# Softmax sums by way of memory, and value matmuls that wait for the last transposed tile

## The chip, the cores and the metric

The kernel runs on one core of one Trainium2 chip. A core has a matmul engine (TensorE, PE in the profile; PEld is its weight load, which runs beside the matmuls), a vector engine (VectorE, DVE), an activation engine (ScalarE, ACT), GpSimd (POOL) and SyncE (SP), which here issues every transfer. The metric is the device time of one launch in microseconds (us). Three runs of the kernel before gave 2056.36, 2057.92 and 2061.26 us; the median is 2057.92.

## The reference, cut to what matters

The program is one step of a two-layer network on 256 context tokens and 1024 latent tokens. Layer A is an attention (8 heads) beside a convolution, layer C a scan over chunks. The change touches the attention's core alone:

```python
s = (einsum('bqhd,bkhd->bhqk', qn, k_nope) + einsum('bqhr,bkr->bhqk', qr, k_rope)) * ATTN_SCALE
p = softmax(s, axis=-1)
o = einsum('bhqk,bkhd->bqhd', p, v)
```

Context tokens attend to the 256 context keys only; latent tokens attend to 512 cached keys and 1024 latent keys. The result of each head is multiplied by a gate before the output projection.

## The kernel before, in words

The program is written as a flow of tile operations. A planner then orders them for each engine: where several are ready at a simulated moment, the one that comes first in the program's text goes first. The engines run their queues strictly in the planned order.

The attention is cut into 80 units: 4 pairs of heads (p), 5 blocks of 256 queries (b; block 0 is the context), 2 heads (j) of the pair, 2 halves (qi) of 128 queries. Four units with the same p and b form a group, whose outputs are stored together; 4 groups are of the context (256 keys, one segment), 16 are full (1536 keys, three segments of 512).

`u_scores` (L599) makes one unit's scores: three matmuls per segment through `mm3` (L118), a maximum on DVE (L617), the exponential on ACT, which also sums (L626), and the sum's reciprocal `ri` on DVE (L630, L631), one value per query, queries on partitions. `u_trans` (L636) transposes the probabilities in packs of four 128x128 blocks (L646) and copies each pack out of PSUM into a `ptile`, on DVE the middle pack (L650), on ACT the others (L652). `u_values` (L655) multiplies the transposed probabilities with the values. The two heads stand in the two column halves of the array and of the PSUM tile `po`: these matmuls use 128 rows by 64 columns (128*64 in the profile), where all others around them use 128*128. A matmul of 32-bit floats shows as two instructions, so a full group has 24 key tiles by heads, 48 value instructions, and a context group 8.

The result lies with queries along the free axis, so the reciprocals must be turned and repeated over the head's 64 rows. Before, TensorE does that, too, in the second half of `po` (L659 to L662), by matmuls of a broadcast `ri` with the identity: 4 matmuls, 8 instructions a group. DVE then multiplies gate and reciprocals (L671), and the values by that (L672); the product goes to memory (L673). Buffers that bind: 5 PSUM banks for scores, 2 for transposes, 1 for `po`; 2 buffers of `prob`; 7 of `ptile`, of which a full group holds 6.

The main loop (L700 to L720) issues the scores of unit i, then the transposes of unit i-1, then, where i mod 4 is 1, the values of the group that ended two units earlier. So in the text the values of a group stand behind the scores of the second unit, and the transposes of the first unit, of the next group. `prep_pair` makes keys and queries of the next pair, with transfers from memory; `conv_norm` finishes the convolution in pieces between the units, mostly on POOL.

Of the kernel before, what the change touches and what calls it, by code (L numbers as in the profile page):

```python
# [10 lines left out]
F32 = mybir.dt.float32  # L11
# [39 lines left out]
def body(nc, tc, d, dbg=None, stop=None):  # L51
    es = ExitStack()
    with es:
        _body(nc, tc, d, es, dbg or {}, stop)


def _body(nc, tc, d, es, dbg, stop):
    V, S, G, PE = nc.vector, nc.scalar, nc.gpsimd, nc.tensor
    dma = nc.sync.dma_start

    def pool(name, bufs=1, space=None, side=None, stack=es):
        kw = {}
        if space is not None:
            kw["space"] = space
        if side is not None:
            kw["side"] = side
        if space is None:
            kw["reuse_waits"] = "tile"
        return stack.enter_context(tc.tile_pool(name=name, bufs=bufs, **kw))
# [5 lines left out]
    sm = pool("sm", bufs=3, side="left")  # L75
# [9 lines left out]
    dp = pool("dp", space=DRAM)  # L85

    def psum(tag="x"):
        tag = tag if tag in ptags else "sd"
        p, n = ptags[tag]
        return p.tile([128, 512], F32, name="ps" + tag, tag=tag, bufs=n)  # L90
# [5 lines left out]
    ident = cp.tile([128, 128], F32, name="ident")  # L96
# [21 lines left out]
    def mm3(ps, lh, ll, rh, rl, start, stop_):  # L118
        PE.matmul(ps, lh, rh, start=start, stop=False)  # L119
        PE.matmul(ps, lh, rl, start=False, stop=False)  # L120
        PE.matmul(ps, ll, rh, start=False, stop=stop_)  # L121

    def after(ins, other):
        tc.add_manual_dep(ins.ins, other.ins.name,
                          mybir.DependencyInfo(mybir.DependencyClass.Sync, mybir.DependencyReason.DATA), reason="group")
# [374 lines left out]
    ap_ = pool("attn", bufs=2, side="right", stack=esB)  # L500
# [9 lines left out]
    vt = ap_.tile([128, 14, 512], F32, name="vt", bufs=1)  # L510
# [82 lines left out]
    for p in range(4):  # L593
        for b in range(5):
            for j in range(2):
                for qi in range(2):
                    units.append((p, b, j, qi))

    def u_scores(u, kq):  # L599
        p, b, j, qi = u  # L600
        ks, qs = kq
        tok = (0 if b == 0 else 256 + 256 * (b - 1)) + 128 * qi
        ci = 0 if tok < 256 else (1 if tok < 768 else 2)
        o = tok - CHUNKS[ci][0]
        segs = [0] if b == 0 else [1, 2, 3]
        qh, ql = qs[(j, ci)]
        mx = sm.tile([128, 4], F32, name="mx", tag="mx", bufs=6)
        sums = sm.tile([128, 4], F32, name="sums", tag="sums", bufs=6)
        nk = sum(KSEG[si][1] for si in segs)
        prob = ap_.tile([128, 1536], F32, name="prob", tag="prob")  # L610
        pss = []
        for x, si in enumerate(segs):
            n = KSEG[si][1]
            kh, kl = ks[(j, si)]
            ps = psum("s")
            mm3(ps[:, :n], qh[:, o:o + 128], ql[:, o:o + 128], kh[:, :n], kl[:, :n], True, True)
            V.tensor_reduce(mx[:, x:x + 1], ps[:, :n], axis=AX.X, op=ALU.max, negate=len(segs) == 1)  # L617
            pss.append((ps, n))
        if len(segs) > 1:
            nm = sm.tile([128, 1], F32, name="nm", tag="nm", bufs=6)  # L620
            V.tensor_reduce(nm, mx[:, :len(segs)], axis=AX.X, op=ALU.max, negate=True)  # L621
        else:
            nm = mx[:, 0:1]
        c = 0
        for x, (ps, n) in enumerate(pss):
            S.activation(prob[:, c:c + n], ps[:, :n], AF.Exp, bias=nm, accum_out=sums[:, x:x + 1])  # L626
            c += n
        ri = sm.tile([128, 1], F32, name="ri", tag="ri", bufs=8)
        if len(segs) > 1:
            V.tensor_reduce(ri, sums[:, :len(segs)], axis=AX.X, op=ALU.add)  # L630
            V.reciprocal(ri, ri)  # L631
        else:
            V.reciprocal(ri, sums[:, 0:1])
        return prob, ri, nk

    def u_trans(u, st, pts):  # L636
        p, b, j, qi = u
        prob, ri, nk = st
        for g in range(0, nk // 128, 4):
            n4 = min(4, nk // 128 - g)  # L640
            if qi == 0:
                pts[(j, g)] = ap_.tile([128, 4, 256], F32, name="ptile", tag="pt", bufs=7)
            dst = pts[(j, g)]
            ps = psum("pt")
            for x in range(n4):
                PE.transpose(ps[:, x * 128:(x + 1) * 128], prob[:, (g + x) * 128:(g + x + 1) * 128], ident)  # L646
            o = dst[:, :n4, qi * 128:qi * 128 + 128]
            p3 = ps[:, :n4 * 128].rearrange("p (k q) -> p k q", q=128)
            if g == 4:
                V.tensor_copy(o, p3)  # L650
            else:
                S.copy(o, p3)  # L652
        pts[("r", j, qi)] = ri

    def u_values(p, b, pts):  # L655
        q0 = 0 if b == 0 else 256 + 256 * (b - 1)
        kts = list(range(2)) if b == 0 else list(range(2, 14))
        po = psum("po")
        for qi in range(2):  # L659
            for j in range(2):  # L660
                PE.matmul(po[64 * j:64 * j + 64, 256 + 128 * qi:384 + 128 * qi],
                          pts[("r", j, qi)].to_broadcast([128, 64]), ident, start=True, stop=True)  # L662
        for x, kt in enumerate(kts):
            for j in range(2):
                h = 2 * p + j
                PE.matmul(po[64 * j:64 * j + 64, 0:256], vt[:, kt, 64 * h:64 * h + 64],  # L666
                          pts[(j, 4 * (x // 4))][:, x % 4, :], start=x == 0, stop=x == len(kts) - 1)
        t2 = ap_.tile([128, 256], F32, name="t2", tag="t2")
        sg = sgs.pop((p, b))
        om = ap_.tile([128, 256], F32, name="om", tag="om")  # L670
        V.tensor_mul(t2, sg, po[:, 256:512])  # L671
        V.tensor_mul(om, po[:, 0:256], t2)  # L672
        dma(mixd[p, :, q0:q0 + 256], om)  # L673

# [25 lines left out]
    for i in range(len(units) + 2):  # L700
        if i < len(units):
            u = units[i]
            if i % 4 == 0:
                sgs[u[:2]] = ap_.tile([128, 256], F32, name="sg", tag="sg")
                dma(sgs[u[:2]], sgd[u[0], :, 256 * u[1]:256 * u[1] + 256])
            state[u] = u_scores(u, kqs[u[0]])
            if i % 20 == 19 and u[0] < 3:
                kqs[u[0] + 1] = prep_pair(u[0] + 1)
        if 0 < i <= len(units):
            v = units[i - 1]  # L710
            pts = done.setdefault((v[0], v[1]), {})
            u_trans(v, state.pop(v), pts)
            if v[2] == 1 and v[3] == 1:
                late_v.append(v)
        if i % 4 == 1 and late_v:
            v = late_v.pop(0)
            u_values(v[0], v[1], done.pop((v[0], v[1])))
        if ci < len(cn) and i % 20 in (1, 3, 5, 7, 9, 11, 13):
            next(cn[ci])
            ci += 1  # L720
        if i == 68:
            esE.close()
            esA.close()
            wps[0] = pool("wpB", bufs=2, side="left")
            hls.append(pool("hlB0", bufs=16, side="left", stack=esH))
            load_mix(0, KORD[:4])
            wao.extend(split_w(d["wao"][m], 8, 128) for m in range(2))
# [161 lines left out]
    def dtile(name, dt=F32, tag=None):  # L889
        return dq.tile([128, HT], dt, name=name, tag=tag or name)  # L890
# [40 lines left out]
    p = dtile("p")  # L931
# [43 lines left out]
    for half in range(2):  # L975
        hs = slice(half * 64, half * 64 + 64)
        for c0 in range(0, 5):
            c = half * 5 + c0
# [561 lines left out]
```

## Time and profile before

| | us |
|---|---|
| median of three runs | 2057.92 |
| the profiled execution, its own time | 2060.95 |
| its span (first to last instruction) | 2059.1 |
| PE busy, of the span | 1993.4 (97%) |
| DVE busy | 1415.9 (69%) |
| ACT busy | 882.3 (43%) |
| POOL busy | 578.7 (28%) |

The mean granted TensorE clock is 0.988 of full speed. PE's busy time counts a matmul from its start to a modelled end, and neighbours overlap; time that PE loses between two instructions can so be hidden in it. The start times in the timeline show it: the distance from one start to the next, less what the instructions need when they follow each other densely.

### The profile page before, as it was taken

The numbers are of one execution on the slowest core, as the hardware profiler recorded it, in microseconds if no ns is written. First come the engines' busy times: TensorE is split into PE (matmuls) and PEld (weight loads), VectorE is DVE, ScalarE is ACT, GpSimd is POOL, SyncE is SP. The second block draws the span as 40 slices with busy tenths as digits, with TensorE's granted clock in tenths as the row PEclk, the third lists the DMA queues.
The fourth block names the chain that finished last, engine by engine and source line by source line (L and its number), as shares of the span: only waits on it lengthen the run. The fifth ranks groups of instructions, "written<-read, shape, count | busy, mean of one in ns | idle before, by whom it ended". The sixth has DMA issues, their size and how long they took to land.

```text
span 2059.1 us, 32474 instructions
## 1 busy us (share of the span) xinstructions
PE 1993.4 (97%) x11830; PEld 1626.0 (79%) x11830; DVE 1415.9 (69%) x2257; ACT 882.3 (43%) x1683; POOL 578.7 (28%) x487
## 2 busy tenths in 40 slices
PE   6999999999999999989999999999999999799997
PEld 3787888777777777868888888888888888589997
DVE  5798798556666673275757876876778587784744
ACT  5411321666566673244544343443334244333531
POOL 1211122212222311563123333333433243342001
PEclk8999999999999999999999999999999999999998
DMA  8434213311122224331566768765866678755442
GB/s 315 181 118 150 54 70 108 115 57 42 57 60 60 77 82 164 140 114 52 142 217 205 229 203 237 208 191 173 244 204 194 179 235 252 220 182 185 145 157 72
DMA packets 273341, 313.57 MB, mean 152 GB/s; under 512 B 21184, under 2 KB 221920, under 8 KB 273184
## 3 DMA queue, kind: packets, MB, share of 16 engines
q1 hardware_dynamic: 273184, 311.51, 48.0%
q8 instruction: 94, 1.54, 0.3%
q14 instruction: 63, 0.52, 0.1%
HBM read 223.38 MB, written 88.05 MB: 151 GB/s over the span
## 4 chain that ended last, share of the span: by engine, by line
PE 90%; DVE 3%; DMA 2%; ACT 1%; issue 1%; SPq 1%; POOL 0%; DVEq 0%; ACTq 0%; POOLq 0%
PE psmm L119 18%; PE psmm L120 18%; PE psmm L121 18%; PE pspo L666 5%; PE pspt L646 4%; PE pssd L1078 3%; PE pss L119 3%; PE pssd L1159 3%; PE pss L121 3%; PE pss L120 3%; PE pssd L1164 2%; PE pssd L1136 2%; PE pssd L1139 2%; PE psx L229 1%; PE pstm L1036 1%
## 5 line engine op out<-in xcount | busy, mean ns | idle before, releaser
L119 PE MATMUL psmm<-hl,wh 128*128 128x512 f32 (+1 forms) x1152 | 428.1, 372 | 4.7 <-ACT wh L114 3.5
L121 PE MATMUL psmm<-hl,wl 128*128 128x512 f32 (+1 forms) x1152 | 423.5, 368 | 4.3 <-POOL wl L115 4.3
L120 PE MATMUL psmm<-hl,wh 128*128 128x512 f32 (+1 forms) x1152 | 423.3, 367 | 0.0
L115 POOL TENSOR_TENSOR wl<-ws,wh 128x1024 fp32r<-128x1024 f32 x89 | 223.6, 2514 | 516.7 <-ACT wh L114 424.5
L119 PEld LDWEIGHTS psmm<-hl,wh 128*128 128x128 f32 x1152 | 219.1, 190 | 37.6 <-ACT wh L114 4.5
L121 PEld LDWEIGHTS psmm<-hl,wl 128*128 128x128 f32 x1152 | 218.8, 190 | 36.9 <-POOL wl L115 6.2
L120 PEld LDWEIGHTS psmm<-hl,wh 128*128 128x128 f32 x1152 | 218.8, 190 | 29.6 <-issue 0.7
L383 DVE SCALAR_TENSOR_TENSOR cacc<-cvin,acw,cacc 128x1295 f32<-128x1295 f32 x120 | 206.9, 1740 | 4.6 <-ACT cacc L378 3.1
L114 ACT CAST wh<-ws 128x1024 fp32r<-128x1024 f32 x109 | 113.6, 1043 | 199.6 <-PE psmm L120 140.3
L848 DVE SCALAR_TENSOR_TENSOR cy<-raw,prm,cy 128x1282 f32<-128x1282 f32 x96 | 157.2, 1637 | 24.6 <-ACT cy L845 17.0
L120 PE MATMUL psmm<-hlo,wh 128*128 128x512 f32 (+3 forms) x480 | 172.1, 359 | 0.0
L119 PE MATMUL psmm<-hh,wh 128*128 128x512 f32 (+3 forms) x480 | 167.8, 360 | 2.5 <-ACT hh L259 2.0
L121 PE MATMUL psmm<-hh,wl 128*128 128x512 f32 (+3 forms) x480 | 170.1, 357 | 0.0
L617 DVE TENSOR_REDUCE mx<-pss 128x1 f32<-128x512 f32 (+1 forms) x208 | 137.3, 668 | 35.2 <-PE pss L121 34.2
L1083 POOL TENSOR_TENSOR st<-st,dec_bc 128x256 f32<-128x256 f32 x104 | 84.3, 815 | 245.2 <-DVE st L1085 165.9
L119 PE MATMUL psmm<-yh,wh 128*128 128x256 f32 (+1 forms) x476 | 147.8, 314 | 5.2 <-ACT yh L1203 3.1
L120 PE MATMUL psmm<-yl,wh 128*128 128x256 f32 (+1 forms) x476 | 148.0, 312 | 0.4 <-DVE yl L1204 0.4
L121 PE MATMUL psmm<-yh,wl 128*128 128x256 f32 (+1 forms) x476 | 147.1, 313 | 0.0
L626 ACT ACTIVATE prob<-pss,nm 128x512 f32<-128x512 f32 x192 | 130.3, 693 | 16.1 <-DVE nm L621 14.2
L646 PE MATMUL pspt<-ident,prob 128*128 128x128 f32 x800 | 121.7, 278 | 4.9 <-ACT prob L626 3.9
L652 ACT COPY ptile<-pspt 128x512 f32<-128x512 f32 (+1 forms) x144 | 81.2, 569 | 104.8 <-PE pspt L646 104.0
L646 PEld LDWEIGHTS pspt<-ident,prob 128*128 128x128 f32 x800 | 92.1, 141 | 40.4 <-ACT prob L626 10.2
(337 smaller groups left out, 4084.5 us busy)
## 6 DMA issues: line engine op xcount, KB each, us to landing
xa<-cmb SPq DMA_DIRECT2D x80, 384.0 KB
wm<-in_wmod_dram SPq DMA_DIRECT2D x48, 512.0 KB
ws<-in_wc_dram SPq DMA_DIRECT2D x40, 512.0 KB
eb<-eyd SPq DMA_DIRECT2D x160, 128.0 KB
ws<-in_wco_dram SPq DMA_DIRECT2D x32, 512.0 KB
cmb<-xt SPq DMA_DIRECT2D x24, 640.0 KB
bx<-cmb SPq DMA_DIRECT2D x72, 192.0 KB
eb<-cmb SPq DMA_DIRECT2D x80, 128.0 KB
```

Source lines behind the costliest of these rows:

```text
L114: S.copy(wh, ws)
L115: (eng or G).tensor_sub(wl, ws, f32(wh))
L119: PE.matmul(ps, lh, rh, start=start, stop=False)
L120: PE.matmul(ps, lh, rl, start=False, stop=False)
L121: PE.matmul(ps, ll, rh, start=False, stop=stop_)
L383: V.scalar_tensor_tensor(cacc[i], cv[:, k:k + CO], acw[:, 31 * i + k:31 * i + k + 1], cacc[i], ALU.mult, ALU.add)
L617: V.tensor_reduce(mx[:, x:x + 1], ps[:, :n], axis=AX.X, op=ALU.max, negate=len(segs) == 1)
L626: S.activation(prob[:, c:c + n], ps[:, :n], AF.Exp, bias=nm, accum_out=sums[:, x:x + 1])
L646: PE.transpose(ps[:, x * 128:(x + 1) * 128], prob[:, (g + x) * 128:(g + x + 1) * 128], ident)
L666: PE.matmul(po[64 * j:64 * j + 64, 0:256], vt[:, kt, 64 * h:64 * h + 64], pts[(j, 4 * (x // 4))][:, x % 4, :], start=x == 0, stop=x == len ...
L848: V.scalar_tensor_tensor(y, raw[:, k:k + RO], ccw[:, 5 * blk + k:5 * blk + k + 1], y, ALU.mult, ALU.add)
L1083: G.tensor_mul(n.rearrange("p (h e) -> p h e", e=64), s.rearrange("p (h e) -> p h e", e=64), dec_ap(u, dr, c))
```

## The change

The matmuls that turn the reciprocals are gone. The four reciprocals of a group go into the four columns of one tile `ri` of 128x4. After the fourth, SP writes that tile to a scratch array `rid` in memory, transposed (512 values of 4 bytes), and reads it back twice, each time as one row of 256 values repeated over 64 partitions, into `rb` (128x256). Gate times `rb` is now computed on POOL. The first value matmul of each head (x == 0) waits for every copy of the group's last unit (j = 1, qi = 1); those behind it carry no such wait of their own, but follow it in the accumulation.

```diff
+    rid = dp.tile([20, 4, 128], F32, name="rid")
...
+        if (j, qi) == (0, 0):
+            rgs[p, b] = sm.tile([128, 4], F32, name="ri", tag="ri", bufs=3)
+        ri = rgs[p, b][:, 2 * j + qi:2 * j + qi + 1]
...
+        if (j, qi) == (1, 1):
+            g = 5 * p + b
+            dma(rid[g].rearrange("c q -> q c"), rgs[p, b])
+            rb = rgs[p, b] = ap_.tile([128, 256], F32, name="rb", tag="rb")
+            for x in range(2):
+                dma(rb[64 * x:64 * x + 64], rid[g, 2 * x:2 * x + 2].rearrange("c q -> (c q)").unsqueeze(0)
+                    .to_broadcast([64, 256]))
...
-            if g == 4:
-                V.tensor_copy(o, p3)
-            else:
-                S.copy(o, p3)
-        pts[("r", j, qi)] = ri
+            cp_ = V.tensor_copy(o, p3) if g == 4 else S.copy(o, p3)
+            if (j, qi) == (1, 1):
+                pts.setdefault("last", []).append(cp_)
...
-        for qi in range(2):
-            for j in range(2):
-                PE.matmul(po[64 * j:64 * j + 64, 256 + 128 * qi:384 + 128 * qi],
-                          pts[("r", j, qi)].to_broadcast([128, 64]), ident, start=True, stop=True)
...
+                if x == 0:
+                    for cp_ in pts["last"]:
+                        after(mm, cp_)
...
-        V.tensor_mul(t2, sg, po[:, 256:512])
+        G.tensor_mul(t2, sg, rgs.pop((p, b)))
```

## Rows read from the trace of the kernel before

**Rows 1.** The page: busy time by engine, and the first shares of the chain
```profile
PE 1993.4 (97%) x11830; PEld 1626.0 (79%) x11830; DVE 1415.9 (69%) x2257; ACT 882.3 (43%) x1683; POOL 578.7 (28%) x487
...
PE psmm L119 18%; PE psmm L120 18%; PE psmm L121 18%; PE pspo L666 5%; PE pspt L646 4%; PE pssd L1078 3%; PE pss L119 3%; PE pssd L1159 3%; PE pss L121 3%; PE pss L120 3%; PE pssd L1164 2%; PE pssd L1136 2%; PE pssd L1139 2%; PE psx L229 1%; PE pstm L1036 1%
```
**Rows 2.** Busy time by stretch, attention stage; PE, PEld, DVE, ACT, POOL, then clock
```profile
380.00:797.00 417.00, 407.50 (x2587) 292.73 (x2585) 263.92 (x648) 260.08 (x646) 97.00 (x68) 1.00 0.19 57
```
**Rows 3.** Waits of PEld, 400 to 790 us: total, times, longest
```profile
PEld pspt L646 <- issue: 9.4, 30, 0.4
PEld pspo L661 <- issue: 7.8, 37, 0.4
PEld pspo L666 <- issue: 7.4, 44, 0.2
```
**Rows 4.** PEld's timeline, one group: start, length, line, count, [idle before]
```profile
447.44 0.19 PEld L661 LDWEIGHTS pspo<-ident,ri 128*64 128x64 f32 x2 [0.17 <-issue]
447.80 0.42 PEld L646 LDWEIGHTS pspt<-ident,prob 128*128 128x128 f32 x4 [0.17 <-ACT prob L626]
...
455.84 0.42 PEld L646 LDWEIGHTS pspt<-ident,prob 128*128 128x128 f32 x4 [0.38 <-ACT prob L626]
456.43 1.49 PEld L666 LDWEIGHTS pspo<-ptile,vt 128*64 128x64 f32 x16 [0.17 <-issue]
458.31 0.19 PEld L119 LDWEIGHTS pss<-kh,qh 128*128 128x128 f32 x1 [0.38 <-issue]
...
460.33 0.63 PEld L666 LDWEIGHTS pspo<-ptile,vt 128*64 128x64 f32 x8 [0.17 <-issue]
461.35 0.42 PEld L646 LDWEIGHTS pspt<-ident,prob 128*128 128x128 f32 x4 [0.38 <-ACT ptile L652]
461.93 1.93 PEld L666 LDWEIGHTS pspo<-ptile,vt 128*64 128x64 f32 x20 [0.17 <-issue]
464.24 0.42 PEld L646 LDWEIGHTS pspt<-ident,prob 128*128 128x128 f32 x4 [0.38 <-issue]
464.83 0.19 PEld L666 LDWEIGHTS pspo<-ptile,vt 128*64 128x64 f32 x2 [0.17 <-issue]
465.40 0.19 PEld L119 LDWEIGHTS pss<-kh,qh 128*128 128x128 f32 x1 [0.39 <-issue]
```
**Rows 5.** PEld's timeline: first and last stretch of 128*64 instructions
```profile
385.85 0.19 PEld L661 LDWEIGHTS pspo<-ident,ri 128*64 128x64 f32 x2 [0.17 <-DVE ri L633]
...
790.53 4.94 PEld L666 LDWEIGHTS pspo<-ptile,vt 128*64 128x64 f32 x46 [0.17 <-issue]
```
**Rows 6.** DVE's timeline of the same group: a reciprocal, a maximum, the last product
```profile
454.47 0.15 DVE L631 RECIPROCAL ri<-ri 128x1 f32<-128x1 f32 x1
454.93 0.69 DVE L617 TENSOR_REDUCE mx<-pss 128x1 f32<-128x512 f32 x1 [0.31 <-PE pss L121]
...
465.97 0.42 DVE L672 TENSOR_TENSOR om<-pspo,t 128x256 f32<-128x256 f32 x1
```
**Rows 7.** POOL's timeline, convolution part: a product of 128x256
```profile
404.57 0.73 POOL L543 TENSOR_TENSOR la<-la 128x256 f32<-128x256 f32 x1
```
**Rows 8.** ACT's timeline around the same group's last transposes
```profile
456.72 0.60 ACT L652 COPY ptile<-pspt 128x512 f32<-128x512 f32 x1
460.44 0.59 ACT L652 COPY ptile<-pspt 128x512 f32<-128x512 f32 x1 [3.12 <-PE pspt L646]
460.92 0.69 ACT L626 ACTIVATE prob<-pss,nm 128x512 f32<-128x512 f32 x1
```
**Rows 9.** SP's and DVE's timeline: a small tile written, read back repeated
```profile
1000.70 0.33 SPq L972 DMA_DIRECT2D decd<-dece  x1
...
1002.05 1.55 DVE L848 SCALAR_TENSOR_TENSOR cy<-raw,prm,cy 128x1282 f32<-128x1282 f32 x1 [0.98 <-DMA decd<-dece]
```
**Rows 10.** The chain of waits, early attention: start, length, what
```profile
378.78 5.04 DMA wsq<-in_wuq_dram
```

More of the change, by code (lines that the diff above doesn't have):

```diff
@@ L597, in _body @@
                     units.append((p, b, j, qi))
+    rgs = {}
+    rid = dp.tile([20, 4, 128], F32, name="rid")
     def u_scores(u, kq):
@@ L627, in u_scores @@
             c += n
-        ri = sm.tile([128, 1], F32, name="ri", tag="ri", bufs=8)
+        if (j, qi) == (0, 0):
+            rgs[p, b] = sm.tile([128, 4], F32, name="ri", tag="ri", bufs=3)
+        ri = rgs[p, b][:, 2 * j + qi:2 * j + qi + 1]
         if len(segs) > 1:
@@ L633, in u_scores @@
             V.reciprocal(ri, sums[:, 0:1])
-        return prob, ri, nk
+        if (j, qi) == (1, 1):
[5 more added lines that the diff above has]
+                    .to_broadcast([64, 256]))
+        return prob, nk
     def u_trans(u, st, pts):
         p, b, j, qi = u
-        prob, ri, nk = st
+        prob, nk = st
         for g in range(0, nk // 128, 4):
@@ L665, in u_values @@
                 h = 2 * p + j
-                PE.matmul(po[64 * j:64 * j + 64, 0:256], vt[:, kt, 64 * h:64 * h + 64],
-                          pts[(j, 4 * (x // 4))][:, x % 4, :], start=x == 0, stop=x == len(kts) - 1)
+                mm = PE.matmul(po[64 * j:64 * j + 64, 0:256], vt[:, kt, 64 * h:64 * h + 64],
+                               pts[(j, 4 * (x // 4))][:, x % 4, :], start=x == 0, stop=x == len(kts) - 1)
+                if x == 0:
+                    for cp_ in pts["last"]:
+                        after(mm, cp_)
         t2 = ap_.tile([128, 256], F32, name="t2", tag="t2")
```

## The prediction

> **What bounds the kernel now.** I read the page first: the busy line and the shares of the chain. PE is busy 97% of the span, and the chain is PE nearly throughout; the value matmuls (L666) alone hold 5% of it [rows 1]. Then the stretch of the attention, 380 to 797 us: PE is busy 407.5 of 417 us at full clock, DVE 264, ACT 260, POOL 97 [rows 2]. So the stage is PE's; the others have a third of it to spare. What PE spends its time on, the busy time doesn't tell, so I went to the waits of the weight loads. They name hardly a partner: the releaser is "issue", 0.17 us ahead of an L661 or L666, up to 0.4 us ahead of the L646 behind one [rows 3]. That is PE waiting for itself, where it goes from 128*128 to 128*64 instructions and back.
>
> The timeline of one group gives the price [rows 4]. Of two stretches, 16 values hold PE 458.31 - 456.43 = 1.88 us and 20 hold it 464.24 - 461.93 = 2.31 us: four more cost 0.43, so one costs 0.107, and 16 of them 1.71. The other 0.17 us of the 1.88 is the way back. The way in: four transposes start at 461.35 and the values behind them at 461.93, 0.58 us; at a like 0.107 us each (0.42 of load time for four) they need 0.43, which leaves 0.15. A stretch of 128*64 instructions so costs 0.32 us beside its own work, and a stray one more: the two values at 464.83 hold PE for 0.57 us, where two out of a dense row would take 0.21, since the array's other half stands empty.
>
> **The part removed: the sums' matmuls and the stray stretches.** Following the weight loads through the stage, I count 109 stretches, from the first at 385.85 to the last at 790.53 [rows 5]: 37 of L661 alone, 20 of L661 with a few L666, 52 of L666. The sampled group has seven of them. From each start to the next instruction's start they add up to 15.8 + 13.3 + 95.5 = 124.6 us. Four contain waits that aren't theirs, 3.6 us together, the largest about 1.35 at the end, where 46 values need 4.94 us and PE is then idle before the next stage [rows 5]. With 109 ways in at 0.15 = 16.4 us, the cost now is 124.6 - 3.6 + 16.4 = 137.4 us.
>
> After the change there are 800 value instructions, 800 x 0.107 = 85.6 us, and n stretches at 0.32. How many is the question. The wait sits on the first matmul of each head only. Behind it all data are there, but the planner prefers what stands earlier in the text, and that is the next group's first unit: of its three packs, the first finds a free `ptile` (6 of 7 are in use), the second needs one that the group's first 16 value instructions release. So I expect the values to be cut about twice: three stretches in each of 16 full groups, one in each of 4 context groups, n = 52. That gives 85.6 + 16.6 = 102.2, a gain of 35 us. The bounds: one stretch a group, n = 20, 92.0 us, a gain of 45; or only the 37 lone sums go and the values stay cut as they are, 15.8 - 2.3 (three of the four waits lie in them) + 37 x 0.15 = a gain of 19. I take 35: it is the count that the buffers give.
>
> The DVE product leaves DVE (20 x 0.42, one row of it [rows 6]); DVE isn't the bound, so it counts zero. On POOL the product of that shape takes 0.73 us [rows 7], 20 x 0.73 = 15 us on an engine that is idle for 320 of 417.
>
> **The part added: the wait for the last copies.** In the sampled group the 16 values start at 456.43; the last copy starts at 456.72 and ends at 457.32 [rows 4, 8]. So the values start 0.9 us later, and what is queued behind them on PE would stand 0.9 us. But the planner can put other work there: the two score segments that now follow at 458.31 (six matmuls, 1.27 us until 459.58) and a pack of the next unit, 0.43. Both are earlier in the text than the values. The cost is between 0 (cover found) and, if PE stood as long as ACT stands in that place now, 3.1 us [rows 8]. That gap on ACT also tells that a stretch of values already starves ACT and DVE today, and that PE doesn't pay for it. I take 0.6 us for each full group, nearer to zero, 16 x 0.6 = 9.6 us.
>
> **The part moved: the way through memory.** One write and two reads, 60 issues of 0.33 us, 20 us of SP's time in 417. SP stands in order: the reads wait for the write, and behind them stand gate loads, stores of products and, at the three pair boundaries, the loads of keys. The nearest row is the scan's small table, written from 128 partitions and read back repeated: issued at 1000.70, and the instruction that waits for it starts at 1002.05 [rows 9], 1.35 us. The other end is the longest load that the chain shows in this stage, 5.04 us [rows 10]. Write and read then take 2.7 to 10.1 us, with three issues and the product 1.7 more: 4.4 to 11.8. The cover: the reciprocal ends at 454.62, the last product starts at 465.97 [rows 6], 11.35 us, of which the gain takes some 2. So the round trip hides up to 9.3 us, and I cost it at zero in a plain group, being nearest to the like table; for SP held up at the pair boundaries I put 1.4 us in all (one small landing; at most 3 x 5.04 = 15). Without the cover DVE would stand in its queue at L672, and the maxima of the next scores behind it.
>
> Here a rule speaks against the change. The row says 1.35 us for a table of 128 short rows [rows 9]. The Trainium skill, page "DMA: Bandwidth & Descriptors", section "Rules for kernel authors", says that a last dimension which isn't contiguous is cut into one descriptor per element; the transposed write would then be 512 pieces. By it, an estimate of four times the 1.35 us, the write takes 5.4 us and the round trip 8.5, still inside 9.3; no run here shows it yet.
>
> **The sum.** 35 gained, 9.6 + 1.4 given back: 24 us off. The profiled execution took 2060.95 us with 2059.1 of span, so 2037 of the same kind; it lies 3.0 us above the median of the runs. From the median 2057.92 I forecast 2034 us. Behind the attention PE goes on at once with dense 128*128 work, so I let the whole 24 us through.
>
> **The rivals.**
> - *The values stand together for good* (n = 20, the wait covered as above): 45 - 11 = 34 us off, 2024. For it: behind the first matmul no wait is left. Against: the earlier units' packs go first.
> - *The change half done*: the planner cuts the values as before, or the cover is thin; 19 us gained against 11 to 22 given back, 2050 to 2061. For it: the planner's order needn't follow real times.
> - *The wait empties the pipe*, slower. One mechanism: the values can't fill holes any more, so PE stands first for the copy (0.9 us) and, when the block is through, no scores have been reduced, so it stands for a maximum 0.69, the exponentials 0.69 at the least, and a matmul 0.69 before them with hand-overs, some 2.3 us. 3.2 x 16 = 51 against 35: 16 us slower, 2074. It decides from 2.2 us of standing per full group on (35 / 16). For it: ACT's 3.1 us hole [rows 8] shows that the units ahead don't reach over a long block. Against: five score banks hold nearly two units, and PE has two units' scores to make.
> - *The round trip is longer than its cover*, slower too: at 11.8 us DVE stands 2.5 us in each full group, 40 us against the net 24: again 2074. It decides from 9.3 + 24 / 16 = 10.8 us on. For it: 4-byte pieces in memory and a single queue. Against: the like table's 1.35.
>
> **How the numbers follow.** The forecast, 2026 to 2048, has 0.56; the values wholly together (2014 to 2026) 0.10, the half-done change 0.18; the emptied pipe 0.10 and the late round trip 0.06. A run tells no change from one below 0.2%, 4.1 us. The half-done case splits into 0.10 faster and 0.08 the same: faster 0.76, same 0.08, slower 0.16. The range leaves out most of the slower cases and reaches from a gain of 44 to no change: 2014 to 2058.
>
> **What would show it.** L661 is gone, and its weight loads. Stretches of L666 should number about 50 (20 in the one rival, over 70 in the half-done case), each with 0.17 us "issue" ahead and 0.38 behind it. L666 should still be 800 instructions. The attention's end, 797 now, should lie at about 773. If L672 on DVE waits for POOL's product or for `rb`, the round trip isn't hidden. If PE's weight loads wait for ACT's copies or exponentials by more than 35 us in the stage, the pipe has run empty. The forecast is wrong if the stage ends after 790, or if the time behind it grows.

## The result

The changed kernel takes 2152.06 us (median of 4, 2149.26 to 2153.24), the kernel before on the same chip 2059.59: a ratio of 1.044, 95% interval 1.0425 to 1.0455. Forecast were 2034 us, in a range from 2014 to 2058. The change costs 92 us where 24 us of gain were expected.

In the changed kernel the line numbers move: scores L620 (maximum) and L629 (exponential), transposes L658, their copies L661, values L672, the write and the reads of the sums L641 and L644, gate by sums L680 on POOL, the last product L681 on DVE.

The page after, busy by engine, and the attention's stretch, which now ends at 883 us instead of 797 (PE, PEld, DVE, ACT, POOL, then the granted clock, DMA share, GB/s), to be set against [rows 1, 2]:

```profile
PE 2003.1 (93%) x11670; PEld 1642.7 (76%) x11670; DVE 1400.1 (65%) x2237; ACT 884.1 (41%) x1683; POOL 593.0 (28%) x507
...
380.00:883.00 503.00, 411.33 (x2416) 304.38 (x2415) 249.47 (x622) 261.88 (x646) 109.68 (x87) 0.91 0.19 52
```

PE is busy as long as before (411 us against 407), in a stretch that is 86 us longer: it stands for 92 us, where it stood for 9.5. The waits of the stage (total, times, longest) say behind whom; `t` is gate by sums, `om` the last product, and the last row is SP's own queue:

```profile
POOL t L680 <- DMA rb<-rid: 276.3, 20, 30.6
DVE om L681 <- POOL t L680: 95.2, 14, 11.9
DVE qq L586 <- POOL ql L588: 41.0, 13, 10.1
PEld pss L119 <- ACT prob L629: 32.0, 30, 6.8
...
SPq L644 <- DMA rid<-ri: 157.5, 20, 9.5
```

Neither of the first two existed before; in [rows 3] PE's longest waits were for itself. A wait is put down to whoever came last, so the 95.2 us hold time in which the values weren't done either. From the end of a group's last value matmul (a modelled end) to the last product pass 67 us over all 20 groups: 32 in the four context groups, 35 in the 16 full ones.

One group, of the context, in time order shows the chain. First SP and POOL (start, length): the write of the sums is issued at 511.65, the first read can go at 519.96, and POOL's product starts at 524.30.

```profile
511.65 0.38 SPq L641 DMA_DIRECT2D rid<-ri  x1
519.96 1.24 SPq L644 DMA_DIRECT2D rb<-rid  x2
...
524.30 0.73 POOL L680 TENSOR_TENSOR t<-sg,rb 128x256 f32<-128x256 f32 x1 [10.46 <-DMA rb<-rid]
```

Then DVE and the weight loads. The group's eight value instructions start at 517.79. The last product is the next instruction in DVE's queue: DVE stands for 6.21 us, and the maxima behind it start at 525.73. PE stands 5.98 us: its next instruction (L184) needs the small tile `rw`, which DVE computes behind the late product, at 527.06. Over the whole stage the longest of PE's waits is another: scores (L119) that wait for exponentials, which stand behind such maxima, 32.0 us above.

```profile
517.79 0.63 PEld L672 LDWEIGHTS pspo<-ptile,vt 128*64 128x64 f32 x8 [0.17 <-issue]
...
518.70 0.16 DVE L178 TENSOR_TENSOR ru<-ru,rv 128x2 f32<-128x2 f32 x1
525.06 0.43 DVE L681 TENSOR_TENSOR om<-pspo,t 128x256 f32<-128x256 f32 x1 [6.21 <-POOL t L680]
...
525.73 0.68 DVE L620 TENSOR_REDUCE mx<-pss 128x1 f32<-128x512 f32 x1
...
527.06 0.15 DVE L179 SCALAR_TENSOR_TENSOR rw<-ru,rr 128x2 f32<-128x2 f32 x1
...
520.76 0.59 PEld L658 LDWEIGHTS pspt<-ident,prob 128*128 128x128 f32 x4
527.33 0.93 PEld L184 LDWEIGHTS pspt<-ident,rw 128*128 128x128 f32 x4 [5.98 <-issue]
```

Over 20 groups the time from the write's issue to the first read's issue is 7.5 to 9.9 us, in the middle 8.4. And behind the standing the granted clock is down for a while: 0.69 of 2.4 GHz from 524 to 530, a mean of both its levels, and 0.50, that is 1.2 GHz, from 527 to 533 (columns as above). The stage's mean of 0.91 stands for some 90 of 503 us at the lower level; before it was 1.00.

```profile
512.00:518.00 6.00, 4.98 (x30) 3.84 (x30) 4.39 (x17) 4.49 (x14) 1.76 (x2) 1.00 0.08 3
...
524.00:530.00 6.00, 2.64 (x10) 2.54 (x11) 3.94 (x11) 2.67 (x8) 0.73 (x1) 0.69 0.14 44
...
527.00:533.00 6.00, 5.64 (x19) 4.93 (x20) 3.75 (x11) 4.67 (x11) 0.00 (x0) 0.50 0.01 2
```

The part of the change that was to win did what it should: mostly two stretches of values in a full group, as at 543 us, and 39 in the stage instead of 109 [rows 4, 5].

```profile
543.03 4.08 PEld L672 LDWEIGHTS pspo<-ptile,vt 128*64 128x64 f32 x38 [0.17 <-issue]
547.49 0.42 PEld L658 LDWEIGHTS pspt<-ident,prob 128*128 128x128 f32 x4 [0.38 <-issue]
548.08 1.05 PEld L672 LDWEIGHTS pspo<-ptile,vt 128*64 128x64 f32 x10 [0.17 <-issue]
```

### The profile page after: what moved, and what is told of

Same layout as the page of the kernel before. It is cut to its first block, busy times and chain, and to the rows that moved or that the text cites. A ratio compares the mean times of both kernels' runs of the same rounds, so it can differ in the third digit from the quotient of the medians.

```text
span 2150.1 us, 32256 instructions
## 1 busy us (share of the span) xinstructions
PE 2003.1 (93%) x11670; PEld 1642.7 (76%) x11670; DVE 1400.1 (65%) x2237; ACT 884.1 (41%) x1683; POOL 593.0 (28%) x507
## 4 chain that ended last, share of the span: by engine, by line
PE 53%; DMA 3%; DVE 3%; issue 1%; ACT 1%; POOL 0%; SPq 0%; DVEq 0%; ACTq 0%; POOLq 0%
PE psmm L119 13%; PE psmm L121 13%; PE psmm L120 13%; PE pssd L1087 3%; PE pssd L1168 3%; PE pssd L1173 2%; PE pssd L1145 2%; PE pssd L1148 1%; DMA rid<-ri 1%; PE pstm L1045 1%; DVE hl L260 1%; DVE ht L253 1%; DMA rb<-rid 1%; PE pssd L119 0%; PE pssd L120 0%
## 5 line engine op out<-in xcount | busy, mean ns | idle before, releaser
L119 PE MATMUL psmm<-hl,wh 128*128 128x512 f32 (+1 forms) x1152 | 429.0, 373 | 11.8 <-DVE raw L822 6.6
L119 PEld LDWEIGHTS psmm<-hl,wh 128*128 128x128 f32 x1152 | 219.9, 191 | 44.6 <-DVE raw L822 7.0
L119 PE MATMUL psmm<-hh,wh 128*128 128x512 f32 (+3 forms) x480 | 167.7, 359 | 1.6 <-ACT hh L259 1.6
L620 DVE TENSOR_REDUCE mx<-pss 128x1 f32<-128x512 f32 (+1 forms) x208 | 136.2, 666 | 38.7 <-PE pss L121 37.7
L629 ACT ACTIVATE prob<-pss,nm 128x512 f32<-128x512 f32 x192 | 130.0, 690 | 67.5 <-DVE nm L624 42.7
L119 PE MATMUL psmm<-yh,wh 128*128 128x256 f32 (+1 forms) x476 | 148.6, 315 | 3.4 <-ACT yh L1212 3.4
L658 PE MATMUL pspt<-ident,prob 128*128 128x128 f32 x800 | 119.3, 283 | 17.7 <-ACT ptile L661 10.6
L119 PE MATMUL pss<-kh,qh 128*128 128x512 f32 (+1 forms) x208 | 99.4, 478 | 37.0 <-ACT prob L629 20.6
L658 PEld LDWEIGHTS pspt<-ident,prob 128*128 128x128 f32 x800 | 98.2, 146 | 46.7 <-ACT ptile L661 13.5
```

## The experiments

Theory A: the sums come back later than the values are done, and DVE and POOL stand in their queues for them. Theory B: the values' wait for the last copies empties the pipe. Ratios are to the kernel before on the same chip, with 95% intervals.

| run | us | ratio | stretches | attention ends | write to read, median us |
|---|---|---|---|---|---|
| before | 2060 to 2062 | 1 | 109 | 797 | - |
| the change | 2152.1 | 1.044 (1.0425-1.0455) | 39 | 883 | 8.4 |
| e1_nowait | 2148.4 | 1.0418 (1.0395-1.0441) | 74 | 880 | 8.3 |
| e2_wait_only | 2062.8 | 1.0015 (1.0003-1.0027) | 96 | 797 | - |
| e3_row16 | 2047.3 | 0.9929 (0.9908-0.9951) | 39 | 782 | 1.4 |
| e4_late_store | 2079.5 | 1.0088 (1.0067-1.011) | 39 | 813 | 8.3 |
| e5_row16_nowait | 2055.5 | 0.9968 (0.9956-0.9981) | 74 | 787 | 1.4 |
| e6_row512 | 2084.5 | 1.0117 (1.01-1.0134) | 32 | 817 | 1.2 |
| e7_sums_wide_wait | 2049.8 | 0.9944 (0.993-0.9957) | 42 | 782 | - |
| e8_sums_wide | 2062.0 | 0.9998 (0.9987-1.0009) | 69 | 796 | - |
| e9_wait_all | 2057.0 | 0.9978 (0.9967-0.9988) | 42 | 792 | - |
| e10_strided | 2060.0 | 0.9994 (0.9983-1.0005) | 39 | 792 | 1.4 |
| e11_piece8 | 2065.1 | 1.0017 (0.9997-1.0038) | 39 | 802 | 4.0 |
| e12_spaced4 | 2069.2 | 1.0041 (1.0025-1.0057) | 39 | 800 | 4.1 |

**One half each.** e1_nowait takes the wait out of the change, e2_wait_only puts it alone into the kernel before.

```diff
-                if x == 0:
-                    for cp_ in pts["last"]:
-                        after(mm, cp_)
```

> The change without the wait of the value matmuls: the sums still go through memory. Theory A (the round trip of the sums is later than the values, and DVE and GpSimd stand in their queues for it): as slow as the changed kernel or nearly, 2110 to 2160 us, with DVE waiting over 70 us at the last product. Theory B (the wait for the last copies empties the pipe): back at or below the kernel before, 2030 to 2060 us.

> The kernel before with the wait of the value matmuls alone; the sums are turned by TensorE as before. Theory A: the wait itself is cheap or a gain, 2025 to 2062 us, with 10 to 20 fewer stretches of narrow matmuls. Theory B: 2110 to 2160 us, TensorE waiting for ACT's copies.

As theory A has it, without the wait the kernel is as slow as with it, and the same wait stands on DVE:

```profile
POOL t L677 <- DMA rb<-rid: 268.4, 19, 31.4
...
DVE om L678 <- POOL t L677: 82.8, 14, 11.4
```

The wait alone changes next to nothing (0.15%; 0.8 us above theory A's range). It also gains nothing: the sums' own narrow matmuls still stand apart, and 96 stretches are left.

**The round trip made short.** e3_row16 is the change with the write as the tile lies. Its sums reach the wrong queries, so it shows the time alone.

```diff
-    rid = dp.tile([20, 4, 128], F32, name="rid")
+    rid = dp.tile([20, 128, 4], F32, name="rid")
...
-            dma(rid[g].rearrange("c q -> q c"), rgs[p, b])
+            dma(rid[g], rgs[p, b])
...
-                dma(rb[64 * x:64 * x + 64], rid[g, 2 * x:2 * x + 2].rearrange("c q -> (c q)").unsqueeze(0)
+                dma(rb[64 * x:64 * x + 64], rid[g, 64 * x:64 * x + 64].rearrange("q c -> (q c)").unsqueeze(0)
```

> The change, but the sums are written to memory as they lie, 128 pieces of 16 bytes instead of 512 pieces of 4, and read back in that order, so each query gets another query's sum; all else is the same. Theory A, with the number of pieces as its cause: from the write's issue to the first read's 1.4 to 3 us instead of 8.2 to 9.5, the round trip inside its cover, 2030 to 2060 us. Theory A with a fixed cost of the way through memory as its cause: still 7 us or more, and over 2100 us. Theory B: 2110 to 2160 us with a short round trip.

This one edit takes 105 us off the changed kernel and turns the loss into a gain of 0.7%. SP's queue, the waits, and the stretch:

```profile
570.91 0.33 SPq L641 DMA_DIRECT2D rid<-ri  x1
572.33 1.08 SPq L644 DMA_DIRECT2D rb<-rid  x2
...
DVE om L681 <- PE pspo L672: 55.7, 15, 7.6
...
DVE om L681 <- POOL t L680: 0.2, 1, 0.2
...
380.00:782.00 402.00, 382.54 (x2415) 285.59 (x2413) 253.42 (x623) 260.49 (x646) 109.83 (x87) 0.99 0.23 64
```

DVE's 95 us for POOL's product are gone (0.2); it still stands 55.7 us there, for the values themselves. PE is busy 25 us less than in [rows 2], and stands 19.5 us instead of 9.5. The changed kernel has the same instructions on PE in this stage: of its 101 us more, 72 are standing, and 29 are busy time, at a mean clock of 0.91 instead of 0.99.

**The long round trip with nothing queued behind it.** e4_late_store moves both products behind the maxima of two units later.

```diff
...
-        G.tensor_mul(t2, sg, rgs.pop((p, b)))
+        t_ = G.tensor_mul(t2, sg, rgs.pop((p, b)))
+        if mx_ is not None:
+            after(t_, mx_)
...
+        if held and (i % 4 == 3 or i == len(units) + 1):
+            u_store(*held.pop(0), lastmx[0] if i < len(units) else None)
```

> The change as it is, but the two products of a group (gate by sums on GpSimd, values by that on DVE) are held back until the scores of two units later have been reduced, so nothing is queued behind a sum that is still on its way. Theory A: the round trip is as long as ever (12 to 14 us), yet DVE's wait at the last product falls below 25 us and the time to 2030 to 2075 us. Theory B: no change, 2110 to 2160 us.

SP's wait for the write is unchanged, DVE's is cut to a quarter, and 73 us come back, which is just above the range that theory A gave. DVE still waits for 7 late sums, once for 11.9 us; that these make up the rest is not shown:

```profile
SPq L645 <- DMA rid<-ri: 158.0, 20, 9.9
...
DVE om L688 <- POOL t L685: 21.9, 7, 11.9
```

So most of the loss, 73 of 92 us, is the place of the late product in two queues, not the transfers themselves. With e1 to e3, theory B is out as its cause.

**What the wait is worth.** With the short write, e5_row16_nowait leaves the wait out again (the diff of e1). e7 and e8 have no way through memory at all: POOL repeats the sums, TensorE turns them in the wide form, with the wait in e7 and without in e8.

```diff
...
+            rp = ap_.tile([128, 256], F32, name="rp", tag="rp")
+            G.tensor_copy(rp.rearrange("p (a b) -> p a b", b=64),
+                          rgs[p, b].rearrange("p a b -> p (a b)").unsqueeze(2).to_broadcast([128, 4, 64]))
...
+            PE.matmul(po[:, 256 + 128 * qi:384 + 128 * qi], rg[:, 128 * qi:128 * qi + 128], ident,
+                      start=True, stop=True)
...
```

> As the run with 128 pieces of 16 bytes (each query gets another query's sum), but without the wait of the value matmuls, so the only difference to that run is the wait. Theory C (the wait groups the values, some 39 stretches instead of some 74, but what it wins, 35 x 0.32 = 11 us, it gives back in standing): 2040 to 2053 us. Theory D (the wait is nearly free and is what wins): 2054 to 2062 us.

> No way through memory: GpSimd repeats the four columns of sums to 128x256, and TensorE turns them by two matmuls in the wide form (4 instructions a group, 20 x 4 x 0.107 = 8.6 us, no change of form), into the second half of the values' bank as before; the values wait for the last copies. Theory C: 39 or so stretches, 2045 to 2058 us. Theory D: 2035 to 2045 us.

> The same without the wait of the value matmuls. Theory C: some 74 stretches and little standing, within 8 us of the run with the wait, 2040 to 2056 us. Theory D: 10 us or more above the run with the wait.

The wait wins 8 us in the one pair (2055.5 to 2047.3) and 12 in the other (2062.0 to 2049.8), with 30 stretches fewer or so. That is theory D for the sign: the wait pays, once nothing else is in its way. Of the sizes, e5 came out as D has it (2054 to 2062), e7 as C has it (2045 to 2058), e8 as D has it (10 us or more above e7): the wait wins, but in e7 less than D gave it. **e7 leaves nothing of the computation out and is below both kernels**, 0.56% under the one before. e9_wait_all keeps the narrow sums, too, and lets them wait with the values:

```diff
...
+                for cp_ in pts["last"]:
+                    after(mm, cp_)
...
```

> The kernel before, sums turned by TensorE in the narrow form as ever, but these matmuls and the values both wait for the group's last copies, so all narrow instructions of a group stand together; nothing goes through memory. Theory D (fewer stretches win, the wait costs little): 35 to 50 stretches instead of 109 and 2038 to 2053 us. Theory C (standing eats it): 2055 us and above.

42 stretches, yet only 4.6 us won: outside theory D's range and inside theory C's. Grouping alone doesn't say what the time is; which of the remaining waits makes the difference to e7 I have not tested.

**Two short writes that keep the order of the sums.** e6_row512 transposes the four columns on TensorE and writes four rows; e10_strided writes as e3 does and lets POOL pick the columns.

```diff
-            dma(rid[g].rearrange("c q -> q c"), rgs[p, b])
+            pr = psum("pt")
+            PE.transpose(pr[0:4, 0:128], rgs[p, b], ident)
+            rt = ap_.tile([4, 128], F32, name="rt", tag="rt")
+            S.copy(rt, pr[0:4, 0:128])
+            dma(rid[g], rt)
```

> The change, but TensorE first transposes the group's four columns of sums (one instruction of the wide form), ACT copies the four rows out, and the write is 4 pieces of 512 bytes in the right order. Theory A (the number of pieces made the round trip long): 1.4 to 3 us from the write's issue to the first read, hidden, 2042 to 2056 us. If a way through memory cost its 8 us with few pieces too: over 2100 us.

```diff
...
+            G.tensor_mul(t2[h].rearrange("p (c q) -> p c q", q=128), sg[h].rearrange("p (c q) -> p c q", q=128),
+                         rb[h, :, 2 * x:2 * x + 2].rearrange("p q c -> p c q"))
```

> The change with the right sums and a short write: 128 pieces of 16 bytes as they lie, read back in one transfer as a row of 512 repeated over 128 partitions, and GpSimd picks the columns in its product (two products of 64 partitions). Theory A: 1.4 to 3 us to the read, DVE's wait at the last product below 10 us, 2042 to 2055 us, below both kernels.

Both writes are short, and both times miss their ranges. In e6 the copy of the rows stands in ACT's queue until TensorE has turned them, with exponentials behind it, and PE's score matmuls wait for these exponentials more than twice as long as in e3, where that row says 15.4. TensorE itself, whose turning instruction shows as 128*4 and not in the wide form, waits for the last sum:

```profile
ACT rt L644 <- PE pspt L642: 24.0, 17, 1.7
...
PE pspt L642 <- DVE ri L636: 7.0, 13, 3.7
...
PEld pss L119 <- ACT prob L629: 34.7, 37, 2.3
```

It looks like the same fault in other queues; no run separates what each of these waits is worth. In e10, POOL is busy 130 us in 380 to 780 against 110 in e3, and DVE waits 23.6 us for POOL's query splits (L588) against 12.0; that this is all of the 13 us between them is not shown.

**Why the write took 8.4 us.** e11_piece8 writes 512 pieces of 8 bytes; e12_spaced4 puts the pieces of 4 bytes at the same addresses as e11's.

```diff
...
-            dma(rid[g].rearrange("c q -> q c"), rgs[p, b])
+            dma(rid[g, :, :, 0].rearrange("c q -> q c"), rgs[p, b])
...
```

> The change with each sum as a pair of which the second is zero: the write has 512 pieces as before, but of 8 bytes, and the reads take twice the bytes. If the number of pieces sets the write's time: 8 to 10 us to the first read, 2130 to 2165 us. If it is that a piece is of 4 bytes only: below 6 us, and below 2100 us.

> As the run with 512 pieces of 8 bytes, but each piece is 4 bytes and the next place of 4 bytes is left free (the scratch is zeroed once before the attention): the addresses step as in that run, the length is as in the change. If the length of 4 bytes sets the write's time: 7.5 to 10 us to the first read, and 2120 to 2165 us. If the spacing does (pieces that share a stretch of memory with 15 others wait for each other; here with 7): 3 to 5 us, and 2055 to 2075 us.

One row pair each, e11 first:

```profile
537.47 0.36 SPq L642 DMA_DIRECT2D rid<-ri  x1
541.42 1.09 SPq L645 DMA_DIRECT2D rb<-rid  x2
```

```profile
535.31 0.36 SPq L644 DMA_DIRECT2D rid<-ri  x1
539.38 1.09 SPq L647 DMA_DIRECT2D rb<-rid  x2
```

The same number of pieces takes half the time when each has 8 bytes of memory to itself, whether 8 or 4 of them are written (2.9 to 4.9 and 2.9 to 5.0 us). So it is neither the number of pieces alone nor their length.

The record of the DMA queues says where in the write the time lies. These are the packets of the changed kernel from 538.0 to 539.4 us, behind a write issued at 538.04, and from there to 546.3, just before its first read at 546.34:

```profile
DMA packets 528, 0.00 MB, mean 2 GB/s; under 512 B 528, under 2 KB 528, under 8 KB 528
...
DMA packets 1, 0.02 MB, mean 2 GB/s; under 512 B 0, under 2 KB 0, under 8 KB 0
```

The 512 pieces, and 16 packets more, are out within 1.4 us, and in the 6.9 us behind them a single packet follows, of 16 KB and not the write's. In the middle of 20 the last piece's packet ends 1.2 us after the issue in the changed kernel, 1.3 in e11 and e12, 1.0 in e3; then 7.0, 2.5, 2.8 and 0.4 us pass until the read is issued. So it isn't sending the pieces that takes long, but what comes between the last packet and the read. Close-packed single values cost more there; that they wait for each other, and how long a stretch of memory they would share, is not shown.

## Why the prediction was wrong

- **The way through memory, costed at zero, is the step that failed.** Its write was sized by the like table, 1.35 us [rows 9], and bounded by the longest load in the stage, 5.04 [rows 10]. It takes 8.4 us, outside both ends. The reads got the same price, though [rows 9] shows a write alone; until POOL starts they take 3.2 to 5.2 us, and in e3 still 3.2 to 4.8. From the write's issue to the end of POOL's product are 13.4 us in the middle (511.65 to 525.03 in the group shown; 12.3 to 14.3 over all), against a cover of 9.3. The rival that named this was the right one, at a chance of 0.06 and with 11.8 us as its worst case.
- The price of the late round trip was put at 2.5 us in each full group, 40 us. For the full groups that was near: the last product starts 2.2 us late on average, 35 us in all. Left out were the four context groups. The cover was read from one full group, but a context group has 8 value instructions, and from its write's issue to its last value are only 3.7 to 7.2 us; there the product is 8.1 us late, 32 us together. Left out, too, were POOL's queue, which stands for the same transfer with the query splits behind it (DVE waits 41.0 us for these, 12.0 in e3), and the clock, 0.91 in the stage, with 29 us more of PE's busy time than in e3.
- The rule of the Trainium skill that I cited against the change ("DMA: Bandwidth & Descriptors", section "Rules for kernel authors": one descriptor per element where the last dimension isn't contiguous) pointed the right way: the estimate from it was 5.4 us. The count agrees with the trace, 528 packets in the 1.4 us behind a write, but the measurement decides on the time: 8.4. Taken as a price by count, the rule would put the 512 pieces of e12 and of the change at one time, and these differ by half.
- The gain in the narrow stretches came out near the forecast, in part by luck. 109 stretches cost 141.0 us with their ways in and foreign waits. In e3, 39 take 101.5 us from start to next start, and 39 x 0.15 = 5.9 of ways in: 107.4, a gain of 33.6 where 35 were forecast. But there are 39 stretches, mostly two in a full group, where 52 were counted; at the prediction's prices 39 would take 98.1 us. Nearly all of the 9.3 us above that are 2.4 of a wait in the last stretch and 6.7 of half-filled pairs: 32 of the 39 stretches end on one, at 0.21 us each. The prediction read such a pair at 464.83 [rows 4] and left it out of the 0.32.
- What is given back was too small. In e3 the attention ends 14.7 us earlier, so some 19 of the 33.6 come back, not 9.6 + 1.4. 10 of them can be seen as PE's standing; that the others were overlap, hidden in PE's busy time before, is not shown.
- That the wait is covered held (e1, e2), and it wins 8 to 12 us in the two pairs of runs in which the sums use no narrow matmuls. DVE's and POOL's own times were right: POOL's product takes 0.73.

## What to carry to other kernels

An operation that waits for a transfer costs its whole lateness to everything queued behind it on its engine, and here on two engines at once. Price the transfer by rows of its own shape (number, length and spacing of pieces), and where there is none, let the worst case go beyond the longest known. Read the cover from the shortest case, too: here that was the context group. Give the late operation a place behind work that doesn't need it, or get the same values without leaving the chip: two wide matmuls did it here for 4 instructions a group, with a copy on POOL. Grouping matmuls by form won 8 to 12 us where the sums used none of the narrow form, and 0 to 5 us where they did.

## What the runs showed of the hardware

- Writing 512 values to memory, from the issue until the read that waits for it was issued: four rows of 512 bytes from 4 partitions 1.2 us, and from 128 partitions 128 pieces of 16 bytes 1.4 us, 512 pieces of 4 bytes packed 8.4 us (7.5 to 9.9), 512 pieces at steps of 8 bytes 4.0 us (of 8 bytes) and 4.1 us (of 4), all medians of 20. In each case the last packet had ended after 0.8 to 1.3 us.
- A change between 128*128 and 128*64 matmuls and back costs 0.32 us beside the work [rows 4], and 0.21 more where the stretch ends on a half-filled pair (32 of 39 stretches in e3). The Trainium skill ("TensorEngine Tiling (Array Packing)", section "Tiling Modes") says that changing the mode drains the engine, and gives no figure; the traces agree that each change costs time, and give this figure.
